# Matmul with batch normalization on one core: one more output block transposed by the DMA, chunk 11 copied dense, and a new order of work

## The chip, the cores and the metric

The kernel runs on one core of one Trainium2 chip. The metric is the device time of one execution in microseconds, as the median of several runs. A profile of one execution lies beside it: what each engine did and when, what it waited for, and what the DMA queues moved.

## The reference

```
def reference(x, weight, gamma, beta, eps):     # x 16x512x1024, weight 1024x768, float32
    y = np.matmul(x, weight)
    mean = np.mean(y, axis=(0, 1), keepdims=True)
    var = np.var(y, axis=(0, 1), keepdims=True)
    y_norm = (y - mean) / np.sqrt(var + eps)
    return (gamma * y_norm + beta).astype(np.float32)
```

x is 8192 rows of 1024 values. Every one of the 768 columns of y is normalized with the mean and variance of all its 8192 rows, so no value of a column can be written before the whole column is computed.

## The kernel before, in words

**Tiles.** The 8192 rows are 16 chunks (`c`) of 512 rows. The 768 columns are six blocks (`nt`) of 128. The depth of 1024 is cut in four pieces (`jw`) of two halves (`e`), so a unit of one chunk and one column block is 8 matmuls of 128x512. Everything multiplied is bf16.

**Loads.** GpSimd (POOL) issues the loads of x and weight, four DMAs for a chunk, which turn float32 into bf16 on the way (lines 387 and 403). VectorE (DVE) transposes them in 32x32 blocks into `xT_sb` (`turn_x`, lines 428 and 435). In most chunks it moves pairs of bf16 as one float32, which is quicker, but leaves the two halves `e` interleaved: a matmul then reads every second element. Chunks 2, 3 and 6 (`SINGLE`) are turned as bf16 and lie dense. For the chunks in `PARTED`, ScalarE (ACT) copies the interleaved chunk to a dense one, `x_pl`, in four pieces (`part_chunk`, line 547). The chunks in `LATE` (12 to 15) are copied so later, by ScalarE or VectorE.

**Two ways of computing.** Columns 0 to 255 are computed with rows on the partitions (`mm_rows`, line 510) for the first 14 chunks, 16 matmuls of 128x256 for a row unit. ScalarE squares each result (659), VectorE adds it to a running sum (662), GpSimd or VectorE adds the square (666), ScalarE keeps the result as bf16 (672). Chunks 14 and 15 of these columns are computed the other way (`ga_unit`, 814). Columns 256 to 767 are column blocks 2 to 5, with columns on the partitions (`mm`, 575): statistics by VectorE (711) and a copy by ScalarE (715), or both by ScalarE with sums (720, 724). When the row part is complete, its totals are formed (871 to 899), the scale and shift are spread over the partitions (903), and the rows are normalized (937, 942) and stored (946).

**Turning the output.** A column block has to be transposed before it is stored. `col_block` does this for two chunks at a time: normalize, turn, store. Its `MODE` says how. With `'pe'`, TensorE (PE) transposes eight 128x128 tiles with the identity (1044), ScalarE copies them out of PSUM (1210). With `'xact'`, a DMA transpose issued by SyncE (SP, 1220) turns them from SBUF to SBUF and ScalarE converts the result to float32 (1232). Some blocks (`RAW`) are turned by the DMA before they are normalized (`raw_turn`, 1106; `raw_block`, 1174 and 1178). The last two chunks of block 4 are held until TensorE's last column unit is done (`held_block`, 1252 and 1255). Block 5 comes last: its statistics are complete only after TensorE's last matmul of `last_unit` (753), then a square root (1311), scale and shift (1324), normalization (1348), transposes, copies (1361) and stores (1364).

**Buffers.** 8 PSUM buffers; 12 buffers for `xT_sb` and `x_pl`; a ring in SBUF for what is loaded and stored.

**What sets the order.** The kernel describes its work as tasks with a planned duration on each engine that may do them, what they depend on, which buffers they take, and a priority (`prio`, a due time). `arrange` plays them when the program is built, with these durations and a model of the DMA (`Wires`): at each step it takes the engine that can begin first, and of the tasks that can begin there about then, that of the lowest `prio`. The result is one fixed order for each engine, written into the program by `seq`. On the chip an engine works through its own order and waits where an input or a buffer isn't ready; nothing overtakes on an engine, and SyncE's queue holds the stores and the DMA transposes in one order. A TensorE column unit can host transposes: one goes behind each of its matmuls.

The lines that name the modes and the chunks:

```
    PARTED, LATE, SINGLE = (4,5,7,8,9,10), (12,13,14,15), (2,3,6)
    MODE = {2:'xact',3:'xact',4:('pe',)*8}
```

Of the kernel before, what the change touches and what calls it, by code (L numbers as in the profile page):

```python
# [9 lines left out]
class Task:  # L10
# [3 lines left out]
    def __init__(self, prio, engines, emit, deps=(), dma=None, uses=(), takes=()):  # L14
        self.prio, self.engines, self.emit, self.deps = prio, engines, emit, list(deps)
        self.dma, self.uses, self.takes = dma, list(uses), list(takes)
        self.end = self.after = None
        self.hosts = 0
        self.count = 1
        self.lock = False  # L20
        self.slack = self.look = 0.0
        for slot in self.uses + self.takes:
            slot.users.append(self)
# [74 lines left out]
class Wires:  # L98
# [4 lines left out]
    def __init__(self):  # L103
        self.free = 4.3
        self.lanes = {"SP": [], "POOL": [], "ACT": []}
# [5 lines left out]
    def send(self, queue, t, hold, took, count):  # L111

        soft = queue == "POOL"
        for _ in range(count):
            t = max(t, self.ready(queue)) + hold / count
            self.free = max(self.free, t + (1.0 if soft else 0.5)) + took / count
            land = self.free + (1.3 if soft else 0.6)
            self.lanes[queue].append(land)
        return t, land


def arrange(tasks, turns, log=None):
# [8 lines left out]
    SEM, LOOK = 0.06, 0.2  # L131
# [36 lines left out]
    while left:  # L168
# [46 lines left out]
        if t.dma:  # L215
            free[e], t.end = wires.send(e, start, occ, t.dma, t.count)
# [11 lines left out]
def kernel(  # L228
# [19 lines left out]
    P = 128  # L248
# [26 lines left out]
    PARTED, LATE, SINGLE = (4,5,7,8,9,10), (12,13,14,15), (2,3,6)  # L275
    MODE = {2:'xact',3:'xact',4:('pe',)*8}
# [98 lines left out]
    STORE, XBAR = 1 / 350.0, 1.25  # L375
# [72 lines left out]
    for kind, n, *n1 in order:  # L448
# [12 lines left out]
        if m0 == M // 2:  # L461
# [5 lines left out]
            t, {"POOL": (2.68 * rows / CH + 0.535 * also, 2.68 * rows / CH + 0.535 * also)}, load_x(m0, rows, slot, between),  # L467
# [5 lines left out]
        for i in range(rows // QR):  # L473
            c, q = divmod(m0 // QR + i, QPC)
            for j0, j1 in ((0, JW // 2), (JW // 2, JW)) if m0 < CH else ((0, JW),):
                new = q == 0 and j0 == 0
                x_ready[c, q, j1] = task(
                    -1000 + t, dve((2.2 if c in SINGLE else 1.16) * (j1 - j0) / JW + 0.02),
                    turn_x(slot, x_slot[c], m0, i * QR // 32, j0, j1, new), [load],
                    uses=[slot] if new else [slot, x_slot[c]], takes=[x_slot[c]] if new else [])  # L480
                if not new:
                    x_ready[c, q, j1].deps.append(x_ready[c, 0, JW // 2 if m0 < CH else JW])
            x_ready.setdefault((c, q, JW // 2), x_ready[c, q, JW])
        if rows % QR:
            t0 = rows // QR * QR // 32
            m1 = m0 + 32 * t0
            c, q = divmod(m1 // QR, QPC)
            x_ready["tile", m1 // P] = task(
                -1000 + t, dve(0.63), turn_x(slot, x_slot[c], m0, t0, 0, JW, False, P),
                [load, x_ready[c, 0, JW]], uses=[slot, x_slot[c]])  # L490
            x_ready[c, q, JW] = x_ready[c, q, JW // 2] = x_ready["tile", m1 // P]
# [157 lines left out]
    def rows_stats(c, ts, slot, t):  # L649
# [30 lines left out]
        s = task((now + 4.2 if c < RC - 2 else 0), {"POOL": (1.36, 1.36 + 0.05), "DVE": (0.62, 0.7)}, add_squares, [a],  # L680
# [124 lines left out]
    def ga_unit(nt, c, q, cols=QR):  # L805
# [26 lines left out]
        b = task(clock[0] - late, dve(0.609 * cols / CH + 0.05), bn, [t], uses=[slot])  # L832
        mine = [h[1] for k, h in ga_half.items() if k[1] == c]
        k = task(clock[0] + 3.4, act(0.48 * cols / CH + 0.03), keep, [b] + mine,
# [3 lines left out]
    for c in range(1, RC):  # L838
        for ts in ([0, 1], [2, 3]):
            rows_unit(c, ts)  # L840
        if c in PARTED:
            part_chunk(c, clock[0] + (4.0 if c < EARLY else 20.0), act(1.05))
# [12 lines left out]
    merges.append(task(U, dve(0.36), merge(0), [k[1] for k in ends], True))  # L855
    merges.append(task(U, pool(0.65), merge(1), [k[2] for k in ends]))
    for h in range(2):
        merges.append(task(U, pool(0.65), more(h), merges[1:]))
# [59 lines left out]
    s1 = task(U, pe(0.9), sums_rows, merges, takes=[tot_slot])  # L918
    se = task(U, dve(0.8), sums_entry, [s1], True, uses=[tot_slot])
    ag = [task(U, dve(0.25), aggregate_rows(a), [se] + [h[0] for k, h in ga_half.items() if k[0] == a]) for a in range(GA)]  # L920
    rt = task(U, {"ACT": (0.2, 0.3)}, root_rows, ag)
    sc = task(U, dve(0.3), scale_rows, [rt], True)
    sr = task(U + 0.1, dve(0.35), shift_rows, [sc], True)
    p0 = task(U, pe(0.45), spread_rows(0), [sc], takes=[a0_slot])
    p1 = task(U, pe(0.45), spread_rows(1), [sr], takes=[a1_slot])
    p1.look = 0.6
    sh = task(U, act(0.3), shift_sbuf, [p1], uses=[a1_slot])


    def rows_out(c, s0, s1, k):  # L930
# [19 lines left out]
        a = task(due, dve(0.3 * n), norm, [p0] + keeps, takes=[slot], uses=[y_row[c], a0_slot])  # L950
        b = task(due + 0.4, dve(0.3 * n) if k in ADDED else pool(0.59 * n), add, [a, p1 if k in ADDED else sh],
                 uses=[slot, a1_slot] if k in ADDED else [slot])
        task(due + 1.0, {"SP": (0.38, 0.4)}, store, [b], dma=n * NA * P * 4 / 1024 / 365.0 * 1.024,
# [14 lines left out]
    def finish_tasks(nt):  # L968
# [41 lines left out]
        if nt in ASTAT:  # L1010
            deps = [task(now + 1.0, {"ACT": (1.2, 1.3)}, total, deps)]
        a = task(now + 1.0, dve(0.5), var, deps)
        b = task(now + 1.0, {"ACT": (0.2, 0.3)}, root, [a])
        if nt > GA:
            return task(now + 1.0, dve(0.55), affine, [b], True)
# [40 lines left out]
    def ga_block(c, due):  # L1056
# [31 lines left out]
        norms = [task(due, dve(0.25), norm_ga(a), [sr] + [h[1] for k, h in ga_half.items() if k[1] == c], True, uses=[yslot])  # L1088
# [5 lines left out]
        task(due, {"SP": (0.38, 0.4)}, store, [d], dma=RT * NA * P * 4 / 1024 / 365.0 * 1.024, uses=[slot])  # L1094
# [4 lines left out]
    def raw_turn(nt, c, due):  # L1099
# [3 lines left out]
        def xbar(eng):  # L1103
# [3 lines left out]
            if not gated:  # L1107
# [8 lines left out]
        b = task(due, {"SP": (1.4, 1.4)}, xbar, [col_end[nt, c + i][1] for i in range(GY)] + [gate], dma=XBAR,  # L1116
                 takes=[slot], uses=[yslot])
        raw[nt, c] = slot, b
# [8 lines left out]
    def raw_spread(nt, fin_task):  # L1127
# [32 lines left out]
        d = task(now, dve(0.35), turn, [fin_task], True)  # L1160
        g = task(now, {"POOL": (0.8, 0.85), "ACT": (0.9, 1.0)}, gather, [d])
        s = task(now, {"POOL": (1.2, 1.25), "ACT": (1.0, 1.1)}, deal, [g])
        t = task(now, act(0.4), keep, [s], takes=[bank])
        raw_aff[nt] = bank, t, s, row[:, 1]

    def raw_block(nt, c, due):
# [18 lines left out]
        a = task(due, dve(1.18), norm_raw, [t, turned], takes=[slot], uses=[bank, rslot])  # L1185
# [5 lines left out]
    def col_block(nt, c, due, fin_task, held=False):  # L1191
# [26 lines left out]
        def xbar(eng):  # L1218
# [3 lines left out]
        b = task(due + 0.5, {"SP": (1.4, 1.4)}, xbar, [a], dma=XBAR,  # L1222
                 takes=[t_slot] + ([slot] if MODE[nt][c // GY] == "xact" else []), uses=[yslot])
        if MODE[nt][c // GY] == "xpool":
# [4 lines left out]
        else:  # L1229
# [4 lines left out]
            d = task(due + 1.0, act(0.9), convert, [b], uses=[slot, t_slot])  # L1234
# [33 lines left out]
    for nt in range(GA, NT - 1):  # L1268
        if nt == NT - 2:
            for i, c in enumerate(LATE):  # L1270
                part_chunk(c, clock[0] + 0.0 + 4.0 * i, {"DVE": (0.63, 0.7), "ACT": (1.05, 1.1)},
# [54 lines left out]
    su = task(E - 5.0, dve(0.5), sum_up, [col_end[nt, c][0] for c in range(C - 2)])  # L1326
# [12 lines left out]
    for c, r0, rows in ends:  # L1339
# [29 lines left out]
        task(due + 0.6 * (n - 1), {"SP": (0.6, 0.6)}, store, [d], dma=count * P * P * 4 / 1024 * STORE * 1.024,  # L1369
             uses=[slot])  # L1370

    order = arrange(tasks, turns)
# [39 lines left out]
```

## Time and profile before

| what | value |
|---|---|
| median of 3 runs | 206.14 us (205.58 to 206.33) |
| span of the profiled execution | 204.1 us |
| median less this span | 2.0 us |
| first real matmul starts | 12.14 us |
| last matmul of the last unit ends | 186.62 us |
| first and last store of the last column block issued | 189.31 and 198.56 us |
| last landing | 203.15 us |
| HBM read, written | 36.71 MB, 25.17 MB |
| ScalarE's apart-copies (line 547) | 32 of 1063 ns |
| TensorE's transposes (line 1044) | 104 of 221 ns, overlapped |
| DMA transposes (lines 1220 and 1106) | 13 and 6 |

The execution's own time isn't measured apart from its profile: the span runs from its first to its last instruction, and about 2 us lie around it in a timed run. A duration in the profile is that of one instruction from start to end. Instructions of one engine overlap a little, so where an engine is busy without a break the distance from start to start is shorter: 0.947 us for an apart-copy of 1063 ns, 0.216 us for a matmul of 371 ns.

### The profile page before, as it was taken

The numbers are of one execution on the slowest core, as the hardware profiler recorded it, in microseconds if no ns is written. First come the engines' busy times: TensorE is split into PE (matmuls) and PEld (weight loads), VectorE is DVE, ScalarE is ACT, GpSimd is POOL, SyncE is SP. The second block draws the span as 40 slices with busy tenths as digits, with TensorE's granted clock in tenths as the row PEclk, the third lists the DMA queues.
The fourth block names the chain that finished last, engine by engine and source line by source line (L and its number), as shares of the span: only waits on it lengthen the run. The fifth ranks groups of instructions, "written<-read, shape, count | busy, mean of one in ns | idle before, by whom it ended". The sixth has DMA issues, their size and how long they took to land.

```text
span 204.1 us, 3510 instructions
## 1 busy us (share of the span) xinstructions
PE 189.3 (93%) x1210; PEld 114.5 (56%) x1210; DVE 159.3 (78%) x250; ACT 146.2 (72%) x260; POOL 124.1 (61%) x150
## 2 busy tenths in 40 slices
PE   7969999999999999999999999999999999997900
PEld 3457554657488888777865444444444445544600
DVE  4031879999999999969989998987999878657900
ACT  2001461368989999899978766999998959956950
POOL 7776954877499989997403999389613312940000
PEclk9999999999999999999999999999999999999965
DMA  4999999999999999999686899899999999999998
GB/s 71 172 199 196 176 196 196 196 197 197 190 193 197 197 196 196 196 197 195 103 181 200 297 339 336 248 301 328 295 322 227 336 303 274 347 343 310 310 347 253
DMA packets 98562, 48.74 MB, mean 239 GB/s; under 512 B 24304, under 2 KB 98032, under 8 KB 98544
## 3 DMA queue, kind: packets, MB, share of 16 engines
q0 software_dynamic: 34624, 18.36, 65.5%
q1 hardware_dynamic: 63920, 30.16, 52.6%
q8 instruction: 9, 0.15, 0.3%
q14 instruction: 9, 0.07, 0.1%
HBM read 36.71 MB, written 25.17 MB: 303 GB/s over the span
## 4 chain that ended last, share of the span: by engine, by line
PE 86%; ACT 3%; DMA 3%; POOL 2%; issue 1%; ACTq 0%; DVE 0%; POOLq 0%
PE y_ps L575 54%; PE y_ps L510 24%; PE y_ps L814 4%; ACT o_sb L1361 3%; DMA ring<-in_x_dram 3%; PE o_ps L1044 1%; POOL ring L403 1%; POOL w_sb L387 1%; PE y_ps L753 1%; PE a_ps L903 1%; PE o_ps L1074 0%; ACTq L1407 0%; PE idle_ps L591 0%; PE tot_ps L871 0%; ACT ring L1252 0%
## 5 line engine op out<-in xcount | busy, mean ns | idle before, releaser
L575 PEld LDWEIGHTS <-w_sb 128*128 128x128 bf16 x520 | 50.3, 97 | 57.6
L575 PE MATMUL y_ps<-xT_sb,w_sb 128*128 128x512 bf16 (+1 forms) x272 | 59.3, 371 | 0.0
L575 PE MATMUL y_ps<-x_pl,w_sb 128*128 128x512 bf16 x248 | 57.4, 379 | 0.0
L403 POOL DMA_DIRECT2D ring<-in_x_dram x76 | 47.2, 626 | 14.4 <-DMA ring<-in_x_dram 5.5
L510 PE MATMUL y_ps<-w_sb,xT_sb 128*128 128x256 bf16 x448 | 50.6, 273 | 1.7 <-DMA ring<-in_x_dram 1.6
L510 PEld LDWEIGHTS <-xT_sb 128*128 128x128 bf16 x448 | 43.5, 98 | 9.4 <-DVE xT_sb L435 2.9
L435 DVE STREAM_TRANSPOSE xT_sb<-ring 128x1024 f32<-128x1024 f32 (+1 forms) x29 | 31.2, 1111 | 14.1 <-DMA ring<-in_x_dram 13.9
L711 DVE BATCH_NORM_STATS2 stats<-y_ps 128x6 f32<-128x512 f32 x46 | 30.9, 687 | 7.7 <-PE y_ps L575 7.2
L715 ACT CAST y_sb<-y_ps 128x512 bf16<-128x512 f32 x51 | 29.0, 593 | 10.4 <-DVE stats L711 6.3
L547 ACT COPY x_pl<-xT_sb 128x1024 bf16<-128x1024 bf16 x32 | 32.8, 1063 | 1.7 <-DVE xT_sb L435 1.7
L942 POOL TENSOR_TENSOR ring<-ring,sum 128x1024 f32<-128x1024 f32 (+1 forms) x11 | 23.8, 2188 | 14.9 <-ACT y_ps L724 10.9
L659 ACT ACTIVATE sq_sb<-y_ps 128x512 f32<-128x512 f32 x28 | 16.3, 610 | 16.2 <-PE y_ps L510 15.9
L666 POOL TENSOR_TENSOR sum<-sum,sq_sb 128x512 f32<-128x512 f32 x20 | 25.6, 1278 | 3.0 <-ACT sq_sb L659 1.7
L662 DVE TENSOR_TENSOR sum<-y_ps,sum 128x512 f32<-128x512 f32 x28 | 18.9, 675 | 6.3 <-ACT sq_sb L659 5.3
L672 ACT CAST y_sb<-y_ps 128x512 bf16<-128x512 f32 x28 | 16.3, 594 | 8.2 <-DVE sum L662 8.0
L1178 POOL TENSOR_TENSOR ring<-ring,sum 128x1024 f32<-128x1024 f32 x6 | 14.8, 2477 | 9.8 <-issue 8.5
L937 DVE TENSOR_TENSOR ring<-y_sb,a_ps 128x1024 f32<-128x1024 bf16 (+1 forms) x16 | 16.7, 1079 | 0.1
L1044 PE MATMUL o_ps<-ident,y_sb 128*128 128x128 bf16 x104 | 13.1, 221 | 1.6 <-DVE y_sb L1348 1.5
L1232 ACT CAST ring<-ring 128x1024 f32<-128x1024 bf16 x13 | 13.8, 1063 | 0.6 <-DMA ring<-y_sb 0.6
L1145 POOL COPY sum<-sum 32x256 f32<-32x256 f32 (+1 forms) x17 | 5.8, 340 | 13.4 <-DVE sum L1142 6.5
L428 DVE STREAM_TRANSPOSE xT_sb<-ring 128x2048 bf16<-128x2048 bf16 x6 | 13.5, 2290 | 0.1
L591 PE MATMUL idle_ps<-idle_sb 128*128 128x512 f32 x18 | 9.6, 688 | 1.5 <-DVE idle_sb L316 1.5
(104 smaller groups left out, 153.7 us busy)
## 6 DMA issues: line engine op xcount, KB each, us to landing
out_dram<-ring SPq DMA_DIRECT2D x37, 512.0 KB, 3.4
ring<-in_x_dram POOLq DMA_DIRECT2D x52, 256.0 KB, 8.8
out_dram<-o_sb SPq DMA_DIRECT2D x6, 512.0 KB, 4.7
ring<-in_x_dram POOLq DMA_DIRECT2D x16, 128.0 KB, 5.9
w_sb<-in_weight_dram POOLq DMA_DIRECT2D x8, 192.0 KB, 6.2
out_dram<-ring SPq DMA_DIRECT2D x6, 256.0 KB, 3.0
ring<-in_x_dram POOLq DMA_DIRECT2D x4, 192.0 KB, 7.8
out_dram<-o_sb SPq DMA_DIRECT2D x3, 256.0 KB, 2.5
```

What stands on the lines that cost most here:

```text
L403: bi = seq(nc.gpsimd.dma_start(x_bf[32 * i:32 * i + 32], src[:, :, KQ * i:KQ * (i + 1)]))
L435: seq(nc.vector.transpose(dst, src[:, :, jw0:jw1]))
L510: seq(nc.tensor.matmul(y_ps[:, s], x_of(c, jw, e, t * P, (t + 1) * P), w_sb[:, jw, e, 0:NA], start=(s == 0 and jw == 0 and e == 0), stop=( ...
L547: seq(nc.scalar.copy(dst, pairs) if eng == "ACT" else ENG[eng].tensor_copy(dst, pairs))
L575: seq(nc.tensor.matmul(y_ps, w_sb[:, jw, e, nt * P:(nt + 1) * P], moving(c, jw, e, q0 * QR, q1 * QR, parted), start=(jw == 0 and e == 0 an ...
L659: seq(nc.scalar.activation(sq_sb[:, 0:n], slot.tile[:, 0:n], AF.Square))
L662: seq(nc.vector.tensor_add(sum1, slot.tile[:, 0:n], sum1))
L666: seq(ENG[eng].tensor_add(acc, acc, state["sq"][:, 0:n]))
L711: seq(nc.vector.bn_stats(dst, slot.tile))
L715: seq(nc.scalar.copy(y(nt, c), slot.tile))
L937: seq(nc.vector.tensor_mul(slot.o, y_row[c].y[:, s0:s1], aff[0][:, None, :].to_broadcast([P, n, NA])))
L942: seq(ENG[eng].tensor_add(slot.o, slot.o, row[:, None, :].to_broadcast([P, n, NA])))
```

## The change

The modes: block 4 of chunks 8 and 9 (entry 4 of the tuple) is turned by the DMA instead of TensorE. Chunk 11 joins `PARTED`: four more ScalarE copies, and its column units read the dense copy. The planned durations of nearly all tasks and the model of the DMA get other numbers. A table `NUDGE` sets the priority of 203 tasks before `arrange` runs. The instructions on the chip are otherwise the same ones, in another order.

```diff
-    PARTED, LATE, SINGLE = (4,5,7,8,9,10), (12,13,14,15), (2,3,6)
-    MODE = {2:'xact',3:'xact',4:('pe',)*8}
+    PARTED, LATE, SINGLE = (4,5,7,8,9,10,11), (12,13,14,15), (2,3,6)
+    MODE = {2:'xact',3:'xact',4:('pe','pe','pe','pe','xact','pe','pe','pe')}
...
-    SEM, LOOK = 0.06, 0.2
+    SEM, LOOK = 0.03, 0.2
...
-            part_chunk(c, clock[0] + (4.0 if c < EARLY else 20.0), act(1.05))
+            part_chunk(c, clock[0] + (4.0 if c < EARLY else 20.0), {"ACT": (0.946, 1.056)})
...
-        b = task(due, {"SP": (1.4, 1.4)}, xbar, [col_end[nt, c + i][1] for i in range(GY)] + [gate], dma=XBAR,
+        b = task(due, TURN, xbar, [col_end[nt, c + i][1] for i in range(GY)] + [gate], dma=XBAR,
                  takes=[slot], uses=[yslot])
+        b.turned = True
...
+    NUDGE = {
+        0: -85, 3: -49, 4: -18, 7: -6, 10: -2, 12: 8, 14: 9, 17: 9.4, 18: 3, 20: 11, 25: 59, 28: 176, 29: 80,
...
+    }
+    for i, prio in NUDGE.items():
+        tasks[i].prio = prio
     order = arrange(tasks, turns)
```

What the built program shows of the new order:

- TensorE: up to chunk 1 nearly as before. Then the first row unit of chunk 2 comes three half units of chunk 1 earlier, and the row units of chunks 4 to 6 come ahead of several columns of chunks 2 and 3. Chunk 11's unit of column block 2 comes right behind the first row unit of chunk 12, while before it came after chunks 4 to 10 of that block. In the later stretches the chunks of a block are taken in another order, and the blocks overlap more.
- Loads: chunk 7 behind chunk 11, and chunk 13 ahead of 12.
- ScalarE: the four copies of chunk 11 stand between the row units of chunks 9 and 12. The gathers for block 4 (line 1145) move to GpSimd.
- VectorE: nine of the late copies instead of eight, ScalarE seven.
- SyncE: the row stores come in another order. The new transpose of block 4, chunks 8 and 9, stands ahead of three stores of block 3 (chunks 12, 2 and 8) and of all stores of block 4; the raw blocks of block 4 come behind its other stores. In the last block the store of the last chunk comes fifth instead of last.

## The prediction

> **What bounds the kernel now.** I read four views, from coarse to fine: the page, who TensorE waited for, the chain of waits, and then single engines in the stretches that the change touches.
>
> The page first: busy times, and the rows of the 40 slices for PE, ACT, the granted clock and the DMA.
>
> ```profile
> PE 189.3 (93%) x1210; PEld 114.5 (56%) x1210; DVE 159.3 (78%) x250; ACT 146.2 (72%) x260; POOL 124.1 (61%) x150
> ...
> PE   7969999999999999999999999999999999997900
> ...
> ACT  2001461368989999899978766999998959956950
> PEclk9999999999999999999999999999999999999965
> DMA  4999999999999999999686899899999999999998
> ```
>
> TensorE is 9 from the third slice to the 37th at a full clock; the DMA engines are 9 nearly everywhere too. The view of TensorE's waits has three lines, and only these:
>
> ```profile
> PE y_ps L510 <- DMA ring<-in_x_dram: 1.6, 1, 1.6
> PE o_ps L1044 <- DVE y_sb L1348: 1.5, 1, 1.5
> PE idle_ps L591 <- DVE idle_sb L316: 1.5, 1, 1.5
> ```
>
> One is at the start, one before the first real matmul (12.14), one behind the last column (188.59). Between 12.14 and 186.85 TensorE never waits as much as the view counts. So a new order can win nothing there: only less TensorE work, or a shorter head or tail, can. The chain of waits gives the prices of that work (start us, us, what):
>
> ```profile
> 27.85 7.23 PE y_ps L575 x32
> 35.08 3.49 PE y_ps L510 x32
> 38.57 6.91 PE y_ps L575 x32
> ...
> 169.34 0.06 PE o_ps L1044
> 169.40 0.22 PE y_ps L575
> ...
> 186.62 0.24 PE o_ps L1044 x4
> ```
>
> **The change, part by part.**
>
> *The block turned by the DMA* (column block 4, chunks 8 and 9). Eight transposes through the identity leave TensorE. From 169.34 to 177.82 the chain holds 32 of them, each behind one matmul: 8.48 us, less 32 matmuls at 6.91/32, leaves 1.57, or 0.049 each. Eight are 0.40 us, all on the path. Added: one DMA transpose (consecutive landings in a full queue show 1.04 to 1.10 us of DMA time) and a ScalarE convert in place of a ScalarE copy (L1232 1063 ns against L1210 1014 ns: nothing).
>
> The row says 0.40 us of TensorE against about 1.1 us of DMA. The Trainium skill, "VectorE: DVE Perf Modes", "The three transpose paths", gives 390 ns for a 128x128 tile on TensorE and 1309 ns by the DMA, and its rules send such a tile to TensorE. By its figures eight tiles would be 3.1 us against 10.5; no row here is near either, so the sum stays with the rows.
>
> *Chunk 11 copied apart.* Its matmuls of column blocks 2 to 5 then read a dense copy instead of every second element. Chunk 1 (interleaved, 7.23 us) and chunk 2 (dense, 6.91) do the same 32 matmuls: 0.32 us saved, all on the path. Added: four ScalarE copies.
>
> The Trainium skill, "SBUF — State Buffer", "Door 1: The DMA port swizzle", says strided reads are free while two or more hits fall in a 16-byte line. Every second bf16 gives four hits, so by it this part saves nothing. The 7.23 against 6.91 disagree.
>
> *The order of TensorE's work.* A wait appears at chunk 2: three half units of chunk 1 (0.904 each, 7.23/8) now stand behind its first row unit, which started at 34.91 and would start at 32.20. Its data come from VectorE:
>
> ```profile
> 30.01 4.50 DVE L428 STREAM_TRANSPOSE xT_sb<-ring 128x2048 bf16<-128x2048 bf16 x2
> ```
>
> Each takes 2.29 (L428's row, 2290 ns); the first ends at 32.31, so TensorE waits 0.11 plus a handoff of 0.06: 0.15 us lost, bounds 0 and 0.3. The next tight load is the twelfth (chunk 11 before, chunk 7 now): turned at 80.12, wanted at 80.18 before, and no earlier now. All later ones have 0.6 us or more if loads land as in this trace.
>
> *The copies of chunk 11.* This is the wait the change adds. Before, column block 2 reached chunk 11 at 112.83. Now it stands right behind the first row unit of chunk 12, at 93.8 by the sum of the unit rows, and needs ScalarE's copy of piece 1. Everything on TensorE is queued behind it: chunk 12's second row unit, the two last chunks, the statistics, all columns. I count ScalarE's queue up to that copy, from start to start of instructions in a row (square 0.489, copy out of PSUM 0.478 to 0.481, keep with sum 0.584, square with sum 0.603, apart-copy 0.947): 26 + 39 + 1 + 1 + 24 of them with the identity's copy are 55.6 us. Before, ScalarE had done 28 squares, 42 copies and 22 apart-copies, 55.0 us, only by 95.3:
>
> ```profile
> 89.85 2.97 ACT L547 COPY x_pl<-xT_sb 128x1024 bf16<-128x1024 bf16 x3
> ...
> 94.81 0.60 ACT L659 ACTIVATE sq_sb<-y_ps 128x512 f32<-128x512 f32 x1
> ```
>
> By 93.8 that was 53.7. So ScalarE must have 1.9 us more behind it than it had. Its busy time by stretch shows where that can come from:
>
> ```profile
> 42.00:60.00 18.00, 15.41 (x23) 1.00 1.55 194
> ...
> 60.00:102.00 42.00, 40.58 (x72) 1.00 1.36 185
> ```
>
> Idle: 2.6 us in 42 to 60, 1.4 in 60 to 102, and 8.9 (12 less 3.06) in 30 to 42. Row units (two ScalarE instructions each) are moved ahead of columns there: by 55.9 us ten are done instead of eight, and thirteen column units instead of sixteen. I take it that the idle time swallows the 1.9: cost 0, bounds 0 and 1.9.
>
> *Everything else.* Chunk 7 is loaded behind chunk 11 and 13 before 12: same bytes, same count. VectorE copies nine instead of eight of the late pieces (602 ns from start to start), in stretches where TensorE has fewer row units to feed. GpSimd takes four gathers from ScalarE. PSUM buffers: before, between a unit's end and the next user of its buffer there were 9 us of TensorE work in the median of the middle stretches, now 6; the shortest are 2.6. An eviction alone takes 1.3 us (L711 687 ns, then L715 593), so it fits unless an engine is late: 0, bounds 0 and 0.5. The tail: the same fifteen or so instructions from the last matmul to the first store; the 256 KB store of the last chunk moves from last to fifth. Landings stand 1.5 us apart for 512 KB from 193.3 on, the DMA is full, and order in a full queue is nothing: 0, bounds -0.5 and +0.5.
>
> **Sum.** -0.40 - 0.32 + 0.15 = -0.57 us. The profiled span is 204.1; the median of 206.14 has 2.0 around it, taken as the same. Span 203.5, time **205.6**. The three runs spread by 0.75, so about 0.5% (1.03 us) is what a measurement can tell from no change.
>
> **Rivals.**
>
> *B, slower: ScalarE is late with chunk 11.* For it: ScalarE is busy 40.58 of 42 us in that stretch, and on the same queue behind the copies stands the square root that the row output waits for. Against: the idle time before 60. It decides once less than 1.9 us of work is brought forward; with none, 205.6 + 1.9 = 207.5. Chance 0.24.
>
> *C, slower: SyncE's queue.* The new transpose waits for block 4's statistics, and SyncE works in order: three stores of block 3 and all of block 4 stand behind it. Block 4's last matmul has 22.1 us of TensorE work behind it (eleven units of 1.73, the last 1.81, 24 transposes); statistics and normalising take 3.0 (687 + 589 + 314 + 880 + 542 ns), so it goes at about 167. Behind it, until the two held stores at 187.5, are 1.1 + 10 x 1.5 = 16.1 us of DMA: done at 184, 3 us to spare. If it goes 4 us late, the tail is 1 us late: 206.6. Chance 0.06. The Trainium skill's rule on 128x128 tiles speaks for this one.
>
> *D, faster: the tail.* The held store issued at 187.53 took 2.75 us to land, an unloaded 256 KB store 2.1 to 2.3, since the last store of block 4 landed at 189.53. If the new order clears that queue first, 0.5 is gained, and if chunk 2's wait is hidden 0.15: 204.9. By the count under C it clears at 184, but the three raw blocks need 2.5 us of GpSimd each (L1178 2477 ns) in a row, which puts their last store about where it was. Chance 0.14.
>
> *E, it doesn't do what it says:* dense reads of chunk 11 bring nothing: 205.6 + 0.3 = 205.9. Chance 0.06. The Trainium skill's rule on 16-byte lines gives this one.
>
> The forecast keeps 0.50, with 205.0 to 206.2 as its own range. **Chances:** faster by over 0.5% (under 205.1): D's greater part and a tail of the forecast, 0.22. Slower by over 0.5% (over 207.2): B with little brought forward, C, and waits of PSUM buffers on top, 0.17. Within: 0.61. The range must reach into D and B: 204.8 to 207.3.
>
> **What would show it.** Right: 96 transposes of line 1044's kind instead of 104 and 280 dense matmuls instead of 248; TensorE's waits still three lines plus at most a few tenths at chunk 2; the last unit's end at about 186.0. Wrong: a wait of TensorE for the apart-copy at about 94 (B); a transpose in SyncE's queue issued after 170 (C); the first output store of the last column less than 2.7 us behind TensorE's last unit, or landings of the held stores under 2.5 us (D).

## The result, and the profile after

The changed kernel takes **210.31 us** (median of 5 runs, 210.13 to 210.73) against 205.87 for the kernel before in the same sessions (205.58 to 206.33): a ratio of 1.022, 95% interval 1.0205 to 1.0235. The forecast was 205.6 with a range up to 207.3; it is slower by 4.4 us, and the prediction was wrong. The profiled execution (210.24 us) has a span of 208.5 us.

The page of the changed kernel, the same rows as were shown of before:

```profile
PE 188.9 (91%) x1186; PEld 115.1 (55%) x1202; DVE 160.9 (77%) x252; ACT 147.2 (71%) x259; POOL 124.5 (60%) x153
...
PE   7979999999999999998999999999999999795800
...
ACT  2000563279989999998957986988899557668830
...
PEclk9999999999999999999999999999999999999795
DMA  5999999999999999999593998899999999999995
```

TensorE has eight transposes less (1202 weight loads against 1210) and yet reaches further: its 9s run to the 34th slice of a longer span, then come 7, 9, 5 and 8. The granted clock is 9 throughout up to the last three slices, as before. ScalarE, which showed 9 9 9 8 9 5 9 9 5 6 9 5 in its last busy slices before, has 8 8 9 9 5 5 7 6 6 8 8 3 now: it waits for something. The DMA row is full to the end. The view of TensorE's waits shows what is new (us in total, times, longest):

```profile
PE o_ps L1054 <- DVE y_sb L1360: 2.2, 2, 1.6
PE y_ps L520 <- DMA ring<-in_x_dram: 1.5, 1, 1.5
PE idle_ps L601 <- DVE idle_sb L326: 1.5, 1, 1.5
PE y_ps L585 <- ACT ring L1221: 1.0, 1, 1.0
PE y_ps L824 <- DVE xT_sb L445: 0.5, 1, 0.5
PE y_ps L520 <- DVE xT_sb L445: 0.3, 1, 0.3
PE y_ps L585 <- ACT y_sb L725: 0.2, 1, 0.2
```

(Lines of the changed kernel are 10 to 12 higher than before.) Four of these lines are not in the kernel before: two for transposed x (at 62.2 and 98.2), one for an eviction (about 147), one of 1.0 us at 180 for a ScalarE copy that itself waited. None is for chunk 11's apart-copy.

**Where the 4.4 us are.** Two numbers of the last column block tell nearly all: when its first store is issued, and how long that store takes to land. The first is set by the engines, from the last matmul through the statistics to the first copy. The second is 1.8 to 2.3 us in the runs below whose DMA queue is clear then, and more by whatever the queue still holds. In the table of DMA issues it is the row of the two 128 KB stores (out<-in, queue, count, KB each, median us to landing; the first of the two alone takes 2.11 and 3.86), for before and after:

```profile
out_dram<-o_sb SPq DMA_DIRECT2D x2, 128.0 KB, 2.1
```

```profile
out_dram<-o_sb SPq DMA_DIRECT2D x2, 128.0 KB, 3.7
```

From that landing on the queue is full in both, and the last store lands 11.7 us later. So the difference in span splits up exactly:

| | before | after | difference |
|---|---|---|---|
| last unit's last matmul ends | 186.62 | 188.79 | +2.17 |
| first store of the last block issued | 189.31 | 191.53 | **+2.22** |
| that store lands after | 2.11 | 3.86 | **+1.75** |
| from there to the last landing | 11.73 | 11.71 | -0.02 |
| from the last landing to the end of the span | 0.92 | 1.36 | **+0.44** |
| span | 204.1 | 208.5 | +4.4 |

The first bold term is lateness of the engines, the second a queue that isn't clear, the third is explained in the last section. The experiments are read in the first two terms.

### The profile page after: what moved, and what is told of

Its sections match the earlier page's. It is cut to its first block, busy times and chain, and to the rows that moved or that the text cites. A ratio compares the mean times of both kernels' runs of the same rounds, so it can differ in the third digit from the quotient of the medians.

```text
span 208.5 us, 3468 instructions
## 1 busy us (share of the span) xinstructions
PE 188.9 (91%) x1186; PEld 115.1 (55%) x1202; DVE 160.9 (77%) x252; ACT 147.2 (71%) x259; POOL 124.5 (60%) x153
## 4 chain that ended last, share of the span: by engine, by line
PE 44%; DVE 16%; DMA 15%; ACT 8%; issue 6%; POOL 5%; ACTq 1%; DVEq 0%; POOLq 0%
PE y_ps L585 25%; PE y_ps L520 13%; DMA ring<-in_x_dram 8%; DMA out_dram<-ring 6%; PE y_ps L824 4%; POOL ring L413 3%; DVE xT_sb L445 2%; DVE stats L721 2%; ACT o_sb L1373 2%; DVE xT_sb L438 2%; DVE sum L672 2%; ACT y_sb L1033 2%; DVE ring L1185 2%; DVE ring L947 2%; DVE x_pl L557 1%
## 5 line engine op out<-in xcount | busy, mean ns | idle before, releaser
L585 PE MATMUL y_ps<-x_pl,w_sb 128*128 128x512 bf16 x271 | 63.6, 379 | 1.7 <-ACT ring L1221 1.0
L585 PE MATMUL y_ps<-xT_sb,w_sb 128*128 128x512 bf16 (+1 forms) x233 | 53.5, 369 | 0.6
L520 PE MATMUL y_ps<-w_sb,xT_sb 128*128 128x256 bf16 x448 | 51.4, 273 | 1.9 <-DMA ring<-in_x_dram 1.5
L445 DVE STREAM_TRANSPOSE xT_sb<-ring 128x1024 f32<-128x1024 f32 (+1 forms) x29 | 31.6, 1112 | 12.6 <-DMA ring<-in_x_dram 12.5
L557 ACT COPY x_pl<-xT_sb 128x1024 bf16<-128x1024 bf16 x35 | 36.0, 1063 | 0.1
L669 ACT ACTIVATE sq_sb<-y_ps 128x512 f32<-128x512 f32 x28 | 17.0, 616 | 24.3 <-PE y_ps L520 22.7
L721 DVE BATCH_NORM_STATS2 stats<-y_ps 128x6 f32<-128x512 f32 x46 | 29.9, 681 | 4.0 <-PE y_ps L585 3.9
L676 POOL TENSOR_TENSOR sum<-sum,sq_sb 128x512 f32<-128x512 f32 x19 | 24.6, 1295 | 5.3 <-ACT sq_sb L669 4.8
L1156 POOL COPY sum<-sum 32x64 f32<-32x64 f32 (+1 forms) x21 | 7.2, 343 | 9.8 <-DVE sum L1153 9.0
L1054 PE MATMUL o_ps<-ident,y_sb 128*128 128x128 bf16 x96 | 10.4, 247 | 2.2 <-DVE y_sb L1360 2.2
L1185 DVE TENSOR_TENSOR ring<-r_sb,a_ps 128x1024 f32<-128x1024 bf16 x6 | 7.2, 1213 | 5.8 <-ACT a_ps L1169 5.2
```

Source lines behind the costliest of these rows:

```text
L445: seq(nc.vector.transpose(dst, src[:, :, jw0:jw1]))
L520: seq(nc.tensor.matmul(y_ps[:, s], x_of(c, jw, e, t * P, (t + 1) * P), w_sb[:, jw, e, 0:NA], start=(s == 0 and jw == 0 and e == 0), stop=( ...
L557: seq(nc.scalar.copy(dst, pairs) if eng == "ACT" else ENG[eng].tensor_copy(dst, pairs))
L585: seq(nc.tensor.matmul(y_ps, w_sb[:, jw, e, nt * P:(nt + 1) * P], moving(c, jw, e, q0 * QR, q1 * QR, parted), start=(jw == 0 and e == 0 an ...
L676: seq(ENG[eng].tensor_add(acc, acc, state["sq"][:, 0:n]))
L721: seq(nc.vector.bn_stats(dst, slot.tile))
```

## The experiments

All ratios are to the kernel before, run on the same chip in turn. "Issue" and "landing" are the two numbers above, in the kernel's profiled execution. That is one execution each: the first real matmul started between 11.40 and 12.82 us in them (12.14 before), and the profiled ones of e6, e9, e10 and e3 were 2.1, 1.9, 1.0 and 0.9 us above their medians. So some tenths of a microsecond in these two columns mean nothing.

| kernel | median us | ratio, 95% interval | issue | landing after |
|---|---|---|---|---|
| before | 205.9 | | 189.31 | 2.11 |
| after | 210.31 | 1.0205 to 1.0235 | 191.53 | 3.86 |
| e1 without the priorities | 209.77 | 1.0142 to 1.0208 | 191.16 | 3.83 |
| e2 both parts, planned anew | 222.15 | 1.0753 to 1.0833 | 196.72 | 4.38 |
| e3 durations alone | 208.29 | 1.0059 to 1.0136 | 192.64 | 1.78 |
| e4 after, block on TensorE | 208.34 | 1.0066 to 1.0171 | 191.44 | 1.94 |
| e5 after, stores cut | 208.49 | 1.0092 to 1.0220 | 190.54 | 3.30 |
| e6 after, matmuls cut | 209.92 | 1.0169 to 1.0273 | 193.15 | 4.00 |
| e7 after, both cut | 209.95 | 1.0156 to 1.0219 | 191.13 | 4.02 |
| e8 after, x transposes ahead | 211.92 | 1.0232 to 1.0323 | 193.26 | 3.94 |
| e9 old order, block | 208.47 | 1.0093 to 1.0185 | 191.44 | 4.01 |
| e10 old order, chunk 11 | 210.76 | 1.0210 to 1.0269 | 195.06 | 2.25 |
| e11 old order, both | 213.90 | 1.0311 to 1.0420 | 195.52 | 4.01 |
| e12 after without chunk 11 | 210.06 | 1.0161 to 1.0215 | 191.91 | 3.81 |
| e13 e9, half in an x buffer | 207.04 | 1.0035 to 1.0079 | 188.88 | 3.31 |
| e14 after, half in an x buffer | 209.75 | 1.0154 to 1.0213 | 190.42 | 4.00 |
| e15 old order, 11 in a row | 211.38 | 1.0222 to 1.0311 | 193.90 | 2.27 |
| e16 new order, neither part | 209.18 | 1.0117 to 1.0176 | 192.65 | 1.98 |
| e17 e13, one store cut | 205.73 | 0.9983 to 1.0010 | 188.88 | 2.17 |
| e18 planner constant | 208.34 | 1.0096 to 1.0151 | 189.64 | 4.12 |

In all of them but e2 the last landing is 11.7 to 12.1 us behind that first landing.

### The change taken apart, the planner run again

Theories. 1: the order that the priorities make costs the time. 2: the two parts do (the block turned by the DMA, chunk 11 copied apart). 3: the new planned durations do, through the order that they give. In e1 to e4 the planner runs again and decides.

e1 leaves out the priorities:

```diff
-    for i, prio in NUDGE.items():
-        tasks[i].prio = prio
```

> The changed kernel with its 203 priorities left out: chunk 11 copied apart, the block turned by the DMA and the new planned durations stay. Theory 1 (the priorities' order costs the time: loads, row units and stores come in an order in which the output stream starts some 3 us later and TensorE ends 2.1 us later): 205 to 206.5 us. Theory 2 (the two parts cost it: one more DMA transpose in a full queue, four more ScalarE copies): 208.5 to 210.5. Theory 3 (the new planned durations cost it): 208 to 210.5 here, and the same in the run with the durations alone.

Measured 209.77. Leaving the priorities out doesn't bring the time back, so theory 1 doesn't hold in this form. It doesn't clear the order that they make, though: without them the planner makes another order, on TensorE 97% that of the kernel before, which may lose as much for reasons of its own. What the changed kernel's order costs is measured in e16.

e2 is the kernel before with the two lines `PARTED` and `MODE` of the change:

> The kernel before with the two parts alone: chunk 11 copied apart and chunks 8 and 9 of column block 4 turned by the DMA; the old planned durations, no priorities. Theory 1 (priorities): 205.2 to 206.2, 0 to 0.7 under the kernel before. Theory 2 (the parts): 208 to 210.5. Theory 3 (durations): 205.2 to 206.2.

Measured 222.15, outside every theory. The planner, with its old durations, answers the two parts with a poor order, even by its own plan, which ends at 219.5 us: no DMA transpose is issued between 105.6 and 146.6, the DMA moves 47 GB/s in the slice from 143 to 149 and the backlog comes at the end. It tells nothing of the parts themselves, and it shows that a run with the planner free never changes one thing alone.

e3 is the kernel before with the changed durations and DMA model, neither part, no priorities:

> The kernel before with the new planned durations alone. Theory 1 (priorities): 205.4 to 206.6. Theory 2 (the parts): 205.4 to 206.6. Theory 3 (durations): 208 to 210.5, from another order of the same work.

Measured 208.29, as theory 3 says: some 2 us are lost (1.2 to 2.8 by the interval) though every unit of work is the same. The queue is clear when the last block starts (1.78); TensorE is late, its last matmul ends at 189.94.

e4 is the changed kernel with `MODE` 4 all `'pe'`:

> The changed kernel with chunks 8 and 9 of column block 4 turned by TensorE again; priorities, durations and chunk 11 as changed. Theory 1 (the order): 209 to 210.7, that is at most 1.1 us of DMA time back in a full queue, less 0.4 us of TensorE. Theory 2 with the transpose as its cost: 206 to 208. Theory 3: 209.5 to 210.7.

Measured 208.34: 2.0 less than the changed kernel, between what theories 1 and 2 gave. The first store is issued at the same time as in the changed kernel (191.44 against 191.53), but lands in 1.94 and not 3.86. So with the block goes the whole second term of the table, and the first stays. Two reservations: the order isn't wholly kept (VectorE and ScalarE take some steps of blocks 4 and 5 in another order, from the normalizing of block 4 on), and e9 and e14 below show that the block can delay the engines too.

### Cutting work near the end

Theory A: the end has two bounds, the first store of the last block (+13.8) and what the queue still holds, and both are late. Theory B: TensorE's late end alone. e5 lets four stores write a quarter of their block, e6 leaves out 12 matmuls, e7 does both:

```diff
-            seq(ENG[eng].dma_start(dst(), slot.o))
+            n = 2 if (nt, c) in ((3, 12), (3, 2), (3, 8), (4, 8)) else count; seq(ENG[eng].dma_start(dst()[:, 0:n], slot.o[:, 0:n]))
...
-                    seq(nc.tensor.matmul(
+                    if nt < NT - 1 or c not in (7, 9, 10, 11) or e == 0 or jw == 3: seq(nc.tensor.matmul(
```

> The changed kernel, but four 512 KB stores that stand one behind another in SyncE's queue from 174.86 to 179 (chunks 12, 2 and 8 of column block 3, chunk 8 of block 4) write 128 KB each; the rest of those blocks is left out. That is 3 x 1.1 us and more of DMA time less ahead of the last column. Theory A (two bounds: the end is 13.8 us behind the first store of column block 5, or later by what the DMA queue still holds then; the changed kernel is late on both): the queue is clear when that store is issued at 190.5 to 191.6, the last landing at 204.3 to 205.4, time 207.0 to 208.6. Theory B (TensorE's late end alone): 209.8 to 210.5.

> The changed kernel, but of the eight matmuls of each of chunks 7, 9, 10 and 11 in column block 5 three are left out: 12 matmuls, 2.6 us of TensorE less at the end. Theory A: TensorE ends some 2 us sooner, but the DMA queue is full from 177 to 207 and holds the end where it is: 209.7 to 210.5. Theory B: the end moves with TensorE, 207.6 to 208.6.

> Both cuts together, stores and matmuls. Theory A: only now do both bounds fall: 205.0 to 206.6. Theory B: the same as the cut of the matmuls alone, 207.6 to 208.6.

Measured 208.49, 209.92 and 209.95. Less TensorE work doesn't help: B falls. Less DMA work helped alone, but the four runs of e5 lie between 208.08 and 210.63, and its interval touches that of the changed kernel. A is half right at most: e7 is outside both expectations, and the queue that A has clear isn't (3.30 in e5, 4.02 in e7). In e7 TensorE ends at 185.69, 3.1 us sooner than in the changed kernel, and then stands:

```profile
PE o_ps L1054 <- DVE y_sb L1360: 4.1, 2, 3.8
```

There is a third bound, VectorE. In the changed kernel it stands idle for 5.2 us at 175 to 180, with evictions of the last block queued up behind:

```profile
180.66 1.22 DVE L1185 TENSOR_TENSOR ring<-r_sb,a_ps 128x1024 f32<-128x1024 bf16 x1 [5.22 <-ACT a_ps L1169]
```

It waits for a 0.4 us ScalarE copy of the raw blocks' scales, which stands behind ScalarE copies that wait in turn for a piece of the output ring. The chain of waits of the changed kernel runs through all of them (start us, us, what; the short pieces between are left out):

```profile
174.13 1.41 DMA ring<-y_sb
175.54 3.21 DMA out_dram<-ring
...
178.85 1.02 ACT ring L1221
...
179.91 1.90 PE y_ps L585 x8
...
183.53 1.21 DVE ring L1185
184.74 3.00 DVE stats L721 x5
...
190.41 1.89 DVE y_sb L1360 x6
```

The first line is the new transpose itself.

### Three VectorE instructions moved

Theory C: TensorE's waits for x at 62.2 and 98.2 come from what stands ahead of the transposes on VectorE. The timeline of the changed kernel shows the first one; L445 at 60.91 is the transpose that TensorE waits for; it ends at 62.15:

```profile
58.89 0.67 DVE L676 TENSOR_TENSOR sum<-sum,sq_sb 128x512 f32<-128x512 f32 x1
60.31 0.69 DVE L676 TENSOR_TENSOR sum<-sum,sq_sb 128x512 f32<-128x512 f32 x1 [0.74 <-ACT sq_sb L669]
60.91 1.24 DVE L445 STREAM_TRANSPOSE xT_sb<-ring 128x1024 f32<-128x1024 f32 x1
```

An addition that waits 0.74 us for ScalarE's square stands ahead of it. e8 moves three transposes ahead of such additions:

```diff
+    for i, j in ((35, 188), (52, 282), (53, 281)):
+        order.remove(tasks[i])
+        order.insert(order.index(tasks[j]), tasks[i])
```

> The changed kernel with three VectorE instructions moved: the transpose of chunk 8's second half goes ahead of the addition of chunk 5's squares that waits 0.74 us for ScalarE, and the two of chunk 14 go ahead of the additions of chunk 12. Nothing else is moved. Theory C (TensorE's waits at 62.2, 0.5 us, and at 98.2, 0.7 us, come from those additions standing ahead of the transposes on VectorE, and everything behind them, the output stream too, is late by that): 208.8 to 209.5, TensorE's start of the last column's transposes and the first store earlier by about 1.2 us. Rival (the loads or the buffers hold those transposes, or the gain is swallowed by the DMA queue): 210.0 to 210.6.

Measured 211.92, above both expectations. The wait at 62 is gone, but that shows little. TensorE reaches this unit 50.02 us after its first matmul, and 50.08 in the changed kernel. In e5, e6, e7 and e14, whose instructions up to there are those of the changed kernel, it takes 49.77 to 51.65, and e14 has no wait there without any move. So when x lands differs from one execution to the next by more than the wait. Behind it TensorE loses 0.6 at 80.9 for chunk 7's x, whose load landed 0.8 us later in this execution, 0.7 at 100 to 102, and 1.2 at 135 for evictions. So C isn't shown: the additions stand where it says, but moving the transposes ahead of them gained nothing.

### One part at a time, in a kept order

Here the planner no longer decides: every engine's order is read from a list, so that a run differs from its base in the part alone.

e9, e10 and e11 keep the order of the kernel before. In e9 TensorE hosts no transpose of chunks 8 and 9, and SyncE issues the DMA transpose right behind their normalizing. In e10 the four copies of chunk 11 stand at the first places behind those of chunk 10 at which a buffer of the x tiles is free. e12 keeps the order of the changed kernel without chunk 11's copies. The edit of e11 is shown, without its list; e9 has the line `MODE` alone, e10 the line `PARTED`:

```diff
-    PARTED, LATE, SINGLE = (4,5,7,8,9,10), (12,13,14,15), (2,3,6)
-    MODE = {2:'xact',3:'xact',4:('pe',)*8}
+    PARTED, LATE, SINGLE = (4,5,7,8,9,10,11), (12,13,14,15), (2,3,6)
+    MODE = {2:'xact',3:'xact',4:('pe','pe','pe','pe','xact','pe','pe','pe')}
...
-    order = arrange(tasks, turns)
+    order = replay(tasks, turns, played)
```

> The kernel before, its order of instructions kept on every engine (played from a list), and of the change the turned block alone: chunks 8 and 9 of column block 4 go through the DMA, issued right behind their normalising. By the prediction's price (8 transposes off TensorE, nothing for the DMA): 205.2 to 206.0, that is 0.4 under the kernel before. Rival (towards the end the DMA queue is full, so that 1.1 us more of DMA work is 1.1 us at the end, less what the queue has to spare): 206.2 to 207.5.

> The kernel before, its order kept, and chunk 11 copied apart alone: its four ScalarE copies stand behind the last copy of chunk 10, two of the row units' copies and statistics between them (nearest places at which a buffer is free). By the prediction's price (dense reads, 0.32 us of TensorE saved, the copies hidden): 205.3 to 206.0. Rival (3.8 us of ScalarE work in a stretch where it is busy 97% of the time make evictions late, and TensorE waits): 206.5 to 209.

> The kernel before, its order kept, with both parts. By the prediction's price: 205.0 to 205.8. Rivals: the sum of what the two single runs lose, 207 to 210. If both single runs are within 0.5 of the kernel before and so is this one, the parts are harmless and the 4.4 us come from the order alone.

> The changed kernel, its order kept, without chunk 11's four copies (its columns read the interleaved tile). If the copies make ScalarE late at 93 to 98 (VectorE's addition of chunk 12's squares and the transpose of chunk 14 behind it, TensorE's wait of 0.7 at 98.2): that wait goes, the first store comes some 0.5 to 1 us earlier, 0.32 us come back as longer reads: 209.3 to 210.2. If the copies cost nothing: 210.3 to 210.8.

Measured 208.47, 210.76, 213.90 and 210.06, the first three above everything that was expected. In the old order the block costs 2.5 us, more than its DMA time, and chunk 11 costs 4.8. Of e9, two lines of the timeline (this execution was 1.9 us above e9's median):

```profile
177.40 1.01 ACT L1210 CAST ring<-o_ps 128x1024 f32<-128x1024 bf16 x1 [3.00 <-DMA out_dram<-ring]
...
178.91 1.22 DVE L1174 TENSOR_TENSOR ring<-r_sb,a_ps 128x1024 f32<-128x1024 bf16 x1 [3.13 <-DMA out_dram<-ring]
```

Both wait for a piece of the output ring that a store has yet to free. The turned block holds one and a half pieces (its bf16 half and its float32 result) from the transpose on; turned by TensorE it holds one piece, from the copy on. Of e10, VectorE's line at chunk 15:

```profile
103.93 2.43 DVE L435 STREAM_TRANSPOSE xT_sb<-ring 128x1024 f32<-128x1024 f32 x3 [4.43 <-ACT x_pl L547]
```

The dense copy takes one of the 12 x buffers. None is left for chunk 15 until chunk 11's four copies are done and its interleaved tile is free. In the changed kernel's order, which loads chunk 7 late and copies chunk 11 early, e12 shows no such cost: 210.06 without the copies and 210.31 with them hardly differ. The 210.06 lies where it was expected if the copies make ScalarE late, but the sign for that isn't there: TensorE's wait for chunk 14's x is still 0.3, and the first store is issued no sooner (191.91).

### What the block and the copies hold

e13 and e14 put the block's bf16 half in an x buffer (free by then) and let the ScalarE convert, not the transpose, take the ring piece; e13 in the old order, e14 in the new. Of e13:

```diff
-        t_slot = Slot(rings, count * P // 2)
+        t_slot = Slot(xts) if nt == NT - 2 else Slot(rings, count * P // 2)
...
-                 takes=[t_slot] + ([slot] if MODE[nt][c // GY] == "xact" else []), uses=[yslot])
+                 takes=[t_slot] + ([slot] if MODE[nt][c // GY] == "xact" and nt < NT - 2 else []), uses=[yslot])
...
-            d = task(due + 1.0, act(0.9), convert, [b], uses=[slot, t_slot])
+            d = task(due + 1.0, act(0.9), convert, [b], uses=[t_slot] + [slot] * (nt < NT - 2), takes=[slot] * (nt == NT - 2))
```

> The kernel before, its order kept, with the turned block as in the run of the block alone (208.47), but its transposed half lies in a buffer of the x tiles and not in the output ring, and its piece of the ring is taken by the ScalarE convert, not already by the transpose. If the ring's pieces are what cost the 2.5 us (in the run of the block alone ScalarE waited 3.0 us and VectorE 3.1 for a store to free one): 206.2 to 207.4, those two waits under 1 us. If the DMA time of the transpose and its place in the queue are what cost: 207.8 to 208.8.

> The changed kernel, its order kept, with the same two edits: the transposed half in an x buffer, the ring piece taken by the convert. If the ring costs: TensorE's wait of 1.0 us at 180 behind a ScalarE copy goes, and 208.6 to 209.6. If DMA time costs (the queue is full from 177 to 207): 209.9 to 210.6.

e13: 207.04, so about 1.4 of the 2.5 us were ring pieces. ScalarE's wait falls to 1.0 and VectorE's to 1.3. TensorE's last unit ends at 186.19 and the first store is issued at 188.88, both 0.43 sooner than before. But 0.31 of that is a first matmul at 11.83 instead of 12.14. Counted from the first matmul, TensorE ends 0.25, 0.12 and 0.35 sooner than before in e9, e13 and e17: the sign of the prediction's 0.40 is there, its size isn't confirmed. And the first store lands in 3.31. e14: 209.75, between the two expectations. TensorE's wait at 180 is gone and the first store is issued 1.1 sooner, but lands in 4.00. The total gains 0.6 at most, and the interval (1.0154 to 1.0213) overlaps that of the changed kernel.

e15 puts chunk 11's copies in a row behind those of chunk 10:

> The kernel before, its order kept, with chunk 11 copied apart as in the run of chunk 11 alone (210.76), but its four ScalarE copies stand in a row right behind chunk 10's last one, so that the last ends some 2.4 us earlier (three copies out of PSUM and statistics of 0.6 to 0.8 us stand no more between them). If the x buffer that they free is what VectorE's transpose of chunk 15 and so TensorE wait for: 208.2 to 209.5, VectorE's wait of 4.4 us down to 2 to 3. If ScalarE's added work as such costs: 210.3 to 211.3.

Measured 211.38, just above the second expectation and not 208.2 to 209.5. VectorE's wait for the buffer fell as expected, from 4.4 to 2.65, but the time didn't follow; TensorE then waited for the last row unit's result, which stood behind 5.9 us of copies on ScalarE:

```profile
PE tot_ps L871 <- ACT y_sb L672: 3.2, 1, 3.2
```

So chunk 11's price in the old order is the buffer and ScalarE's queue, one or the other being last; the expectation had only the buffer.

e16 is the changed kernel's order with neither part, and completes the table:

> The changed kernel's order with neither part: block 4 wholly turned by TensorE, chunk 11 not copied apart. If the order costs by itself what is left (parts in this order: 2.0 for the block, 0.25 for chunk 11): 207.8 to 208.6. If the parts account for all: 205.5 to 206.5.

| us | neither | block | chunk 11 | both |
|---|---|---|---|---|
| order of before | 205.9 | 208.47 | 210.76 | 213.90 |
| order of after | 209.18 | 210.06 | 208.34 | 210.31 |

(The entry for chunk 11 in the lower row is e4.)

Measured 209.18, above its expectation. **The new order by itself costs some 3 us**, all as TensorE's lateness (issue at 192.65, queue clear). The waits for transposed x, a ring piece and an eviction that TensorE shows between its first and its last matmul are these:

```profile
PE y_ps L520 <- DVE xT_sb L445: 1.2, 1, 1.2
PE y_ps L585 <- ACT ring L1221: 0.4, 1, 0.4
PE y_ps L585 <- ACT y_sb L725: 0.2, 1, 0.2
PE y_ps L824 <- DVE xT_sb L445: 0.2, 1, 0.2
```

They add up to 2.0. From its first matmul to the last one TensorE takes 3.0 us longer than before, so about 1 us is in no wait that the view counts. What in the order makes each of them isn't shown; e8 was the one attempt at it.

On top of the order the block costs 0.9 (e16 to e12, intervals overlap) to 2.0 us (e4 to after, clear of them). e4 and e16 have the same order, which behind block 4's statistics isn't quite that of e12 and the changed kernel, so the two differences hold a little of the order too. Chunk 11 makes -0.8 and +0.25, neither of which these runs can tell from zero. For both parts together the new order is better than the old one by 3.6 us.

### The last microsecond of the block, and the order as such

e17 is e13 with one 512 KB store writing 128 KB:

> The run with the turned block's half in an x buffer, old order (207.04), with one store less three quarters: chunk 14 of column block 3 writes 128 KB of its 512, the rest is left out; that is 1.1 us of DMA time, as much as the transpose adds. If the 1.0 us that this kernel stands above the one before is DMA time: 205.3 to 206.1, the queue clear again when the last column's first store is issued, and TensorE's 0.4 us shows. If it is something else: 206.6 to 207.2.

Measured 205.73, ratio 0.9996 (0.9983 to 1.0010). So the remaining 1.0 goes with 1.1 us of DMA time, as far as one cut shows; the shorter store also frees its ring piece sooner, and that wasn't tried apart. The last landing is 0.38 sooner than before; the span is the same 204.1, since the end takes 0.4 longer (last section). In e13 that end is part of the sum as well: its span is 1.2 longer than before, that is 1.1 of DMA time and 0.4 at the end, less the 0.4 by which its first store is issued sooner.

e18 changes no work at all:

```diff
-    SEM, LOOK = 0.06, 0.2
+    SEM, LOOK = 0.05, 0.2
```

> The kernel before with neither part, old durations, no priorities: only the planner's handoff constant is 0.05 us and not 0.06. TensorE's order is nearly the same (99% alike), VectorE's 86% and ScalarE's 80%, about as far from before as with the new durations (83% and 76%). If another order of those two engines is enough to cost the 2.3 us that the new durations cost: 207.3 to 209. If the durations' values matter: 205.6 to 206.6.

Measured 208.34. A planner constant moved by 0.01 us costs as much as the new durations. So a loss of 2 us needs no new durations; another order of VectorE, ScalarE and SyncE is enough. The place is another one: in e18 TensorE is on time (last matmul 186.23) and the queue is late (4.12), in e3 it is the reverse. What in e3's order makes TensorE late wasn't followed further than its waits for x. The planner doesn't see these losses. Its own plan ends at 204.65 us for the kernel before, 204.92 for e18, 203.93 for e3 and 202.72 for the changed kernel: it puts the changed kernel 1.9 us ahead, and on the chip it is 4.4 behind.

## Why the prediction was wrong, step by step

Two steps failed, and both are terms that the sum put at nothing.

- **"Everything else ... 0, bounds 0 and 0.5": the larger failure.** The new order cost some 3 us by itself (e16). "A new order can win nothing there" was right as far as it goes (no run with another order was faster than before), but it was taken for "costs nothing". In the changed kernel's profile the lateness shows as waits of TensorE that the kernel before doesn't have: for transposed x at 62 and 98, where additions that wait for ScalarE stand ahead of the transposes, for an eviction at 147, and at 180 behind a full ring. The prediction had looked at when loads land, and not at what stands ahead of each transpose on VectorE; its "0.6 us or more" of slack was taken from the order of before. What in the new order causes each wait stays open.
- **"Added: one DMA transpose ... nothing": the other failed step.** Its own numbers said about 1.1 us of DMA time, and the page said that the DMA is 9 nearly everywhere. The prediction weighed TensorE's time as path and DMA time as cover, though the stores that end the kernel go through that queue. Measured in the old order: 1.1 us of DMA time (e13 to e17), and about 1.4 us for ring pieces (e9 to e13), a resource that the prediction didn't look at. In the new order the block costs 0.9 to 2.0.
- **"Eight are 0.40 us, all on the path":** right in sign. With the order kept, TensorE's end came 0.1 to 0.35 sooner, counted from its first matmul (e9, e13, e17).
- **Rival C named the second of these steps, with a wrong size and a chance of 0.06.** It counted "it goes at about 167 ... done at 184, 3 us to spare". The transpose was issued at 174.13, its own sign ("after 170"). Its data were normalized by 170.12, 3 us after the 167; the other 4 us it stood in SyncE's queue behind twelve transposes and stores issued from 156 on, which C had not added up. Behind it stood what C had counted, and the held stores landed from 194 on. Of the first term of the table, 2.2 us, C said nothing.
- **"The copies of chunk 11":** no wait at 94, cost 0, as forecast. ScalarE did take work forward as the prediction had it: 16.11 us busy in the stretch below instead of 15.41, and 3.53 instead of 3.06 from 30 to 42. The copy of piece 1 is the one at 92.64:

```profile
42.00:60.00 18.00, 16.11 (x24) 1.00 1.55 192
```

```profile
92.64 1.09 ACT L557 COPY x_pl<-xT_sb 128x1024 bf16<-128x1024 bf16 x1
```

That holds for an order that makes room for the copies. In the old order the part costs 4.8 (e10) through the x buffers and ScalarE's queue; rival B looked at the queue and not at the buffer. The 0.32 us of dense reads is real as a duration: chunk 11's unit of block 5 takes 1.73 (181.63 to 183.36) where it took 1.81 before (177.65 to 179.46), and there are four such units. In the total it can't be seen.
- **"0.15 at chunk 2":** none seen; the row unit started at 32.04, without a wait that the view counts.
- **"The tail: 0":** the held stores took 4.5 us to land and not 2.5 or 2.75 as under D. That is the same full queue, and not a term of its own.
- **Smaller slips:** TensorE's row has 6 in the third slice and 7 in the 37th, so it is 9 from the fourth to the 36th. The transposes' landings in the profile of before stand 0.85 to 1.09 apart, not only 1.04 to 1.10. What lies around the span is 1.7 to 1.8 us in the executions that have both times, not 2.0. None of these changes the result.

## What to carry to other kernels

In a kernel with two full resources, work taken off one and given to the other is paid there, so write it at its full price unless that queue is shown clear when the end begins. Here the landing time of the first store of the last stage showed it in one line. Ask of every moved step which buffer it holds, and from when to when. A written-out order is part of what was measured: a new one has to be priced like a change of its own, since orders whose plans end within 0.3 us of each other differed by 2.6 us on the chip (before and e18), and the waits that one execution shows are not all there in the next.

## What the runs showed of the hardware that was not expected

- **The end of the program depends on which semaphore is last.** From the last landing to the end of the span it is 0.92 to 1.02 us in the seven kernels with 88 DMAs on SyncE's queue (before, e3, e4, e10, e15, e16, e18), and 1.35 or 1.36 in the thirteen with 89. SyncE waits there on eight semaphores in a fixed order, 0.06 us apart: with 88 only the last of the eight waits comes behind the last landing, with 89 all eight do, and seven more waits are the 0.44 us of the table. It cost e17 its gain. That the count alone shifts it fits (eleven rounds of eight), but wasn't tried by itself.
- **A DMA transpose is slower for its bytes than a store.** In the full queue a 512 KB store takes 1.50 us (349 GB/s) and one of 256 KB 0.75; a transpose of 256 KB of bf16 from SBUF to SBUF takes 0.85 to 1.10 (238 to 308 GB/s). The Trainium skill, "Advanced Engine Details and Errata", "X-Bar Transpose (TRN2)", has transposes as fast as regular DMAs; these rows disagree.
- **The queue stops near the end.** In every profile a store between 178 and 191 lands 2.6 to 4.1 us after the one before it instead of 1.5 (before: 179.25 to 182.08; after: 184.82 to 187.46); e7, e9 and e11 have two such gaps, and in e9 and e11 the first of them is a store issued only 0.4 us ahead of the landing before it. What the stop is wasn't looked into.
